# An encoder's FFN on one Trainium2 core: input normalised on the chip, eleven of 22 up chunks by seven products, convolution from PSUM, residual and some low parts by accumulating DMA

## The chip, the core and the metric

The kernel runs on one core of a Trainium2 chip. The metric is the device time of one execution in microseconds (us). The engines of the core work side by side: TensorE (PE) multiplies matrices into PSUM, VectorE (DVE) and ScalarE (ACT) work element by element, GpSimd (POOL) does small things and issues some DMAs, SyncE (SP) issues the loads. Each engine takes its instructions in a fixed order that is set when the kernel is built; semaphores make it wait for data of another engine.

## What is computed

The reference is an encoder trunk of two layers over one sequence of 512 tokens with 1024 features, in float32. Layer 0 mixes tokens by a gated linear attention, layer 1 by a grouped softmax attention with rotary positions. Each layer ends in a gated FFN with a convolution of width 3 over the tokens. Its core, cut from the reference:

```
def conv_ffn(h, w_up, w_conv, b_conv, w_down):
    u = h @ w_up                                  # 1024 -> 2 x 2816
    u = conv over 3 neighbouring tokens, one filter per feature, + b_conv
    val, gate = jnp.split(u, 2, axis=-1)
    return (jax.nn.silu(gate) * val) @ w_down     # 2816 -> 1024

x = x + mixer(rmsnorm(x, norm_mix[i]))
x = x + conv_ffn(rmsnorm(x, norm_ffn[i]), w_up[i], w_conv[i], b_conv[i], w_down[i])
```

The change bears on the FFN of both layers.

## The kernel before

**Layout.** Activations lie with features on the 128 partitions and the 512 tokens along a row, so x is eight tiles of 128 x 512 (`x[c]`, L112). Products of float32 are made from two parts of reduced width, a high part (a copy to fp32r) and a low part (the value minus its high part): `mm3` (L359) does high x high, high x low and low x high. Every weight and every activation that PE reads is thus split first, the high part by a copy on ACT, the low part by a subtraction on DVE. For some tiles the low part is made by the DMA: ACT writes the negated high part, and `flush` (L191) issues a DMA on the POOL queue that adds the full value to it (L194). The class `Weights` (L115) keeps the order of all weight pieces; `piece` (L210) hands one out and makes further ones ahead of their use. A strip is 128 x 2048 floats (1 MB), loaded on the SP queue (L136) into one of two buffers (`raw`); a piece is a quarter of the FFN's seven-product strips or half of another.

**The up projection.** An FFN has 22 chunks of 128 value features and their 128 gate features. A plain chunk (`plain_up`, L785) is two tiles, value and gate, each 8 k-steps of `mm3` with 512 columns (`feature_steps`, L365). The input is x times the norm's weight, split; the division by each token's root mean square is done afterwards, by a multiplication with `norm.R` (L803), a tile that holds this factor for every token. `act_up` (L857) then does the convolution (ACT for the middle tap and the bias, L864; DVE for the two outer taps, L865 and L866), silu on ACT (L868) and the product on DVE (L869).

**Seven products.** Six chunks a layer (SEVEN, L49) and most of the down projection use a scheme of Strassen and Winograd: a 2 x 2 block product with seven products instead of eight. Token halves of 256 columns are the blocks on one side, and pairs of 128-row blocks on the other. `seven_up` (L824) has the chunk's products; `go(i, r, ...)` runs the product i over four pairs, 12 matmuls of 128 x 256 each (`product`, L806, matmul at L815), into PSUM tiles r1 to r5. Products accumulate onto one another: r2 starts as a copy of r1, r3 as a copy of r2 (ACT, L831 and L835). `begin_up` lets a chunk's first product run inside the chunk before it. The weights' sums are made on the chip by `summed` (L151), the input's differences by `prepare_input` (L899), called after chunks 0 to 3.

**The down projection.** Chunks 0 to 15 give eight pairs, which `prepare` (L878) turns into the seven right-hand operands each. `down_part` (L921) runs after the first tile of chunk 9 for the first four pairs and of chunk 17 for the other four (DOWN_AFTER, L46), in four groups of seven products, and adds its results to x on DVE (L951, L958 to L962). Chunks 16 to 21 are multiplied plainly at the end (PLAIN, L43; L1002).

**What sets the order.** The text of the kernel gives the order of preference, and a scheduler in the build orders each engine's instructions by it and by estimated readiness. Buffers are counted by tag: PSUM has three banks of `acc`, two of `s`, two of `pt`, one of `po`; in SBUF `wh` and `wl` (split weights) have three each, beside a `ring` buffer of the size of two.

## Time and profile before

| | |
|---|---|
| device time, median of 3 runs | 1104.91 us (1104.68 to 1105.5) |
| profiled execution, first to last instruction (span) | 1103.4 us |
| profiled execution's own time | not given apart from its span; median less span is 1.5 us |
| PE busy | 1096.4 us, 6212 matmuls |
| DVE busy | 870.1 us, 1441 instructions |
| ACT busy | 633.5 us, 1034 instructions |
| POOL busy | 97.9 us |
| granted TensorE clock | 1.000 |

In the lines below, L815 is line 815 of the kernel before. A line of a group names the line, the engine, the operation, what it writes and reads by the program's names with the shape, the count, then busy us, the mean duration of one in ns, and the idle time of the engine just ahead of them with what ended it. A line of the timeline starts with the start time and the duration in us. A line of the waits gives total us, times and the longest. A line of a stretch gives its ends, its length, and for each engine busy us and the number of instructions, then the granted clock, the DMA share and GB/s. Durations of successive instructions on one engine can overlap.

### The profile page before, as it was taken

To read this page: it belongs to the slowest core of one execution; us is meant where nothing else is said; L and a number is where in the kernel's file an instruction comes from. 1 tells how busy PE (TensorE), PEld (TensorE's weight loads), DVE (VectorE), ACT (ScalarE), POOL (GpSimd) and SP (SyncE) were. 2 spreads that over 40 slices of the span, in tenths; PEclk is the share of its full clock that TensorE was granted. 3 is DMA by queue.
4 is the path that set the end of the run, shared out by engine and by line. 5 is a ranking of instruction groups with operands and counts; after the bars stand their busy time and mean duration, and the time that the engine had idled before them with its cause. 6 is when DMAs were issued, how large, how long until landed. Compare 5 with 4: busy or idle time off the path is not lost.

```text
span 1103.4 us, 16108 instructions
## 1 busy us (share of the span) xinstructions
PE 1096.4 (99%) x6212; PEld 960.6 (87%) x6212; DVE 870.1 (79%) x1441; ACT 633.5 (57%) x1034; POOL 97.9 (9%) x106
## 2 busy tenths in 40 slices
PE   9999999999999999999999999999999999999998
PEld 7888888888889988899888888788888998889987
DVE  6785775669998789987964578766999878997893
ACT  5565343446656556666664777645665655665660
POOL 0100222000000000000004343000000000000000
PEclk9999999999999999999999999999999999999999
DMA  6322222222516434364457765422151643445542
GB/s 232 134 96 89 79 100 77 77 77 80 169 45 175 129 98 140 124 173 115 140 152 182 181 178 152 163 77 81 72 166 50 167 134 97 138 129 143 145 134 77
DMA packets 33149, 136.91 MB, mean 124 GB/s; under 512 B 4016, under 2 KB 4528, under 8 KB 22704
## 3 DMA queue, kind: packets, MB, share of 16 engines
q1 hardware_dynamic: 21072, 102.16, 27.1%
q0 software_dynamic: 7104, 25.17, 11.6%
q10 hardware_dynamic: 4896, 8.55, 2.1%
q8 instruction: 49, 0.80, 0.3%
q14 instruction: 28, 0.23, 0.1%
HBM read 100.21 MB, written 2.10 MB: 93 GB/s over the span
## 4 chain that ended last, share of the span: by engine, by line
PE 92%; DVE 4%; DMA 2%; ACT 1%; issue 0%; POOL 0%; ACTq 0%; DVEq 0%; SPq 0%
PE r L815 24%; PE up L361 10%; PE up L362 10%; PE up L363 10%; PE vg L393 8%; PE op L419 8%; PE dn L363 2%; PE dn L361 2%; PE dn L362 2%; PE o L687 1%; DMA ring<-p 1%; PE av L393 1%; PE pt L1191 1%; PE A L361 1%; PE q L361 1%; PE in L620 1%
## 5 line engine op out<-in xcount | busy, mean ns | idle before, releaser
L361 PE MATMUL up<-xhl,wh 128*128 128x512 f32 x512 | 199.9, 390 | 0.0
L362 PE MATMUL up<-xhl,wh 128*128 128x512 f32 x512 | 199.5, 390 | 0.0
L363 PE MATMUL up<-xhl,wl 128*128 128x512 f32 x512 | 199.3, 389 | 0.0
L204 ACT ACTIVATE wh<-raw 128x1024 fp32r<-128x1024 f32 x108 | 114.1, 1057 | 128.8 <-PE up L362 34.0
L205 DVE TENSOR_TENSOR wl<-raw,wh 128x1024 fp32r<-128x1024 f32 x108 | 132.0, 1223 | 30.2 <-ACT wh L204 29.8
L815 PE MATMUL r<-gu,wh 128*128 128x256 f32 x640 | 116.6, 283 | 0.3 <-ACT r L950 0.3
L363 PEld LDWEIGHTS up<-xhl,wl 128*128 128x128 f32 x512 | 96.1, 188 | 20.2
L362 PEld LDWEIGHTS up<-xhl,wh 128*128 128x128 f32 x512 | 96.2, 188 | 19.2
L361 PEld LDWEIGHTS up<-xhl,wh 128*128 128x128 f32 x512 | 96.2, 188 | 19.2
L815 PEld LDWEIGHTS r<-gu,wh 128*128 128x128 f32 x640 | 99.7, 191 | 0.8 <-ACT r L950 0.5
L194 POOL DMA_DIRECT2D wl<-raw x44 | 38.9, 883 | 675.5 <-ACT r L935 195.3
L864 ACT ACTIVATE y<-u,cw 128x512 f32<-128x512 f32 x88 | 68.9, 809 | 47.4 <-DVE u L803 27.1
L815 PE MATMUL r<-gu,wl 128*128 128x256 f32 x320 | 90.4, 283 | 0.0
L393 PE MATMUL vg<-wh,xhl 128*128 128x512 f32 x256 | 80.5, 394 | 0.2 <-DVE wh L202 0.2
L865 DVE SCALAR_TENSOR_TENSOR y<-u,cw,y 128x511 f32<-128x511 f32 x88 | 64.4, 750 | 12.0 <-ACT y L864 12.0
L419 PE MATMUL op<-oT,wh 128*128 128x512 f32 x256 | 71.8, 394 | 0.6 <-ACT p L1155 0.6
L866 DVE SCALAR_TENSOR_TENSOR y<-u,cw,y 128x511 f32<-128x511 f32 x88 | 64.0, 748 | 0.5
L815 PEld LDWEIGHTS r<-gu,wl 128*128 128x128 f32 x320 | 61.1, 191 | 0.0
L393 PEld LDWEIGHTS vg<-wh,xhl 128*128 128x128 f32 x256 | 48.5, 190 | 10.5 <-ACT sq L335 0.5
L419 PEld LDWEIGHTS op<-oT,wh 128*128 128x128 f32 x256 | 47.3, 188 | 11.0 <-ACT p L1155 0.9
L815 PE MATMUL r<-xhl,wh 128*128 128x256 f32 x288 | 53.3, 283 | 0.0
L815 PE MATMUL r<-gu,ring 128*128 128x256 f32 x384 | 50.8, 281 | 0.0
(264 smaller groups left out, 2475.7 us busy)
## 6 DMA issues: line engine op xcount, KB each, us to landing
raw<-in_w_up_dram SPq DMA_DIRECT2D x42, 1024.0 KB, 4.8
wl<-raw POOLq DMA_DIRECT2D x44, 512.0 KB, 4.6
raw<-in_w_down_dram SPq DMA_DIRECT2D x22, 1024.0 KB, 4.8
raw<-in_w_vg_dram SPq DMA_DIRECT2D x6, 1024.0 KB, 4.9
ring<-p ACTq DMA_DIRECT2D x22, 256.0 KB, 3.3
raw<-in_w_kq_dram SPq DMA_DIRECT2D x4, 1024.0 KB, 4.8
raw<-in_w_gout_dram SPq DMA_DIRECT2D x4, 1024.0 KB, 4.8
raw<-in_w_aout_dram SPq DMA_DIRECT2D x16, 256.0 KB, 4.2
```

What stands on the lines that cost most here:

```text
L194: pool.dma_start(lo.bitcast(F32), r, accum_op=ALU.add)
L204: act.activation(hi[:, sl], r[:, sl], AF.Copy)
L205: dve.tensor_tensor(lo[:, sl], r[:, sl], hi[:, sl].bitcast(F32), ALU.subtract)
L361: mm(ps, wh, mh, start=start, stop=False)
L362: mm(ps, wh, ml, start=False, stop=False)
L363: return mm(ps, wl, mh, start=False, stop=stop)
L393: mm(ps[j][:, :width], hl[k][i == 2][:, j * P : (j + 1) * P], (wl if i == 1 else wh)[:, sl], start=k == 0 and i == 0, stop=k == KC - 1 and ...
L419: mm(pss[ng][n], wt[:, sl], mv, start=k == 0 and i == 0, stop=k == KC - 1 and i == 2)
L815: mm(dst, w[:, sl], m, start=start and j == 0 and a == 0, stop=j == len(pairs) - 1 and a == 2, skip_group_check=True)
L864: act.activation(y, u, AF.Identity, scale=w(1), bias=w(3))
L865: dve.scalar_tensor_tensor(y[:, 1:], u[:, : S - 1], w(0), y[:, 1:], ALU.mult, ALU.add)
L866: dve.scalar_tensor_tensor(y[:, : S - 1], u[:, 1:], w(2), y[:, : S - 1], ALU.mult, ALU.add)
```

## The change

In the FFN of each layer:

- **Input.** After chunk 0 the new `rescale` makes x times norm weight times R, four tiles of 128 x 1024, splits them (high part and negated copy on ACT, low part by accumulating DMA) and keeps them as `fresh`. Chunks 0 to 3 still use the old input and the multiplication by R; from chunk 4 on (SWITCH) the input is `fresh` and the multiplication is gone.
- **Convolution.** For those plain chunks the convolution reads the PSUM tile itself (`u = ps`).
- **Seven products.** SEVEN grows from 6 to 11 chunks: 7, 8, 10, 11, 13, 14, 16, 18 to 21. The order within a chunk becomes 6, 7, 5, 3, 4, the next chunk's first product, 2 (it was 6, 7, 2, 5, the next chunk's first, 4, 3), the gate tile is convolved ahead of the value tile, and the results need no R.
- **Differences of the input** are made in place in the scaled tiles, split by ACT and accumulating DMA, after chunks 3, 4 and 5, into buffers of the tag `xhl`.
- **Operands of the down projection**: four of the eight pairs (Q_DMA) get their low parts by DMA.
- **Residual**: a down group's results are gathered in SBUF and added to x by accumulating DMA.
- **Weights**: the third quarter of a seven-product strip gets its low part on DVE, no longer by DMA; loads come in half strips, four buffers, requested up to three pieces ahead; `wh` and `wl` have four buffers each and the `ring` buffer goes; more pieces are made ahead (UPA, PA).

In the attention layers, what used `ring` takes one buffer each of `wh` and `wl`. The diff, cut to what the prediction speaks of:

```diff
-SEVEN = (5, 11, 14, 18, 19, 21)
+SEVEN = (7, 8, 10, 11, 13, 14, 16, 18, 19, 20, 21)
+UPA = 3
+PA = 4
+LOADS = 3
+SWITCH = 4
+INPUT_AT = {3: (0, 1), 4: (2,), 5: (3,)}
+Q_DMA = (2, 4, 5, 6)
+NR = 4
+NH = 4
+NL = 4
...
+        def fetch(self, src, i, h):
+            key = (id(src), i, h)
+            if key in self.loaded:
+                return self.loaded.pop(key)
+            t = pair("raw", NR, F32, "raw")
+            n = 2 if any(src is a and i < m for a, m in self.fine) else 1
+            for q in range(n):
+                w = 2 * S // n
+                sync.dma_start(t[:, q * w : (q + 1) * w], src[i, :, h * 2 * S + q * w : h * 2 * S + (q + 1) * w])
+            return t
+        def load(self, key):
+            src, i, h = key
+            if (id(src), i) in self.sums:
+                if (id(src), i) not in self.strip:
+                    self.strip[id(src), i] = [self.fetch(src, i, 0), self.fetch(src, i, 1)]
+            else:
+                k = (id(src), i, h)
+                if k not in self.loaded:
+                    self.loaded[k] = self.fetch(*key)
...
+        def low_dma(self, hi, lo, r):
+            act.activation(hi, r, AF.Copy)
+            act.activation(lo, r, AF.Copy, scale=-1.0)
+            self.pending.append((lo, r))
...
             if h == 1:
                 dve.tensor_tensor(a11, a21, a11, ALU.add)
-                r = raw[:, : 2 * S]
-            elif h == 2:
-                r = raw[:, 2 * S :]
-            else:
-                r = tmp("sq", "sum4")
-                dve.tensor_tensor(r, a11, a12, ALU.add)
-                hi, lo = (sp.tile([P, S], F32R, tag="sq", bufs=3, name=nm(n)) for n in ("wh4", "wl4"))
-                act.activation(hi, r, AF.Copy)
-                self.last = dve.tensor_tensor(lo, r, hi.bitcast(F32), ALU.subtract)
+                hi, lo = self.two()
+                self.split(hi, lo, t1)
                 return hi, lo
-            if h == 1:
-                t = sp.tile([P, 4 * S], F32R, tag="ring", bufs=1, name=nm("ring"))
-                hi, lo = t[:, : 2 * S], t[:, 2 * S :]
-            else:
-                hi, lo = pair("wh", 3, F32R, "wh"), pair("wl", 3, F32R, "wl")
             if h == 2:
-                act.activation(hi, r, AF.Copy)
-                act.activation(lo, r, AF.Copy, scale=-1.0)
-                self.pending.append((lo, r))
-            else:
-                act.activation(hi, r, AF.Copy)
-                dve.tensor_tensor(lo, r, hi.bitcast(F32), ALU.subtract)
+                hi, lo = self.two()
+                self.split(hi, lo, t3)
+                return hi, lo
+            r = tmp("sq", "sum4")
+            dve.tensor_tensor(r, a11, a12, ALU.add)
+            hi, lo = (sp.tile([P, S], F32R, tag="sq", bufs=3, name=nm(n)) for n in ("wh4", "wl4"))
+            act.activation(hi, r, AF.Copy)
+            self.last = dve.tensor_tensor(lo, r, hi.bitcast(F32), ALU.subtract)
...
+            for key in self.todo[:LOADS]:
+                self.load(key)
...
+        scaled, fresh = [], []
+        def rescale():
+            for p in range(KC // 2):
+                xr = big(F32, "xr")
+                for i in range(2):
+                    c = 2 * p + i
+                    dve.scalar_tensor_tensor(xr[:, i * S : (i + 1) * S], x[c], norm.weight(c), norm.R, ALU.mult, ALU.mult)
+                hi, lo = big(F32R, "nh"), big(F32R, "nl")
+                W.low_dma(hi, lo, xr)
+                scaled.append(xr)
+                fresh.extend((hi[:, i * S : (i + 1) * S], lo[:, i * S : (i + 1) * S]) for i in range(2))
         def plain_up(m):
             pss = []
             for t in range(2):
                 ps = bank("s" if t else "acc", "up")
-                feature_tile(*W.half(up[layer], 2 * m + t, ahead.get((m, t), 1)), norm.hl, ps)
+                feature_tile(*W.half(up[layer], 2 * m + t, max(UPA, ahead.get((m, t), 1))), norm.hl if m < SWITCH else fresh, ps)
                 pss.append(ps)
                 if t == 0 and m not in DOWN_AFTER:
                     begin_up(m + 1)
@@ -798,15 +837,18 @@
                     norm.tokens()
                 elif m == 0:
                     norm.rows()
-            for ps in pss:
-                u = tmp("u", "u")
-                dve.tensor_tensor(u, ps, norm.R, ALU.mult)
-                yield u
+                    rescale()
+            for t, ps in enumerate(pss):
+                u = ps
+                if m < SWITCH:
+                    u = tmp("u", "u")
+                    dve.tensor_tensor(u, ps, norm.R, ALU.mult)
+                yield t, u
         def product(pieces, src, strip, pairs, i, dst, start):
             h, o = PLACE[i]
             if h not in pieces:
-                pieces[h] = W.piece(src, strip, h, 3)
+                pieces[h] = W.piece(src, strip, h, PA)
             wh, wl = pieces[h]
             for j, p in enumerate(pairs):
                 sl = slice(o + j * P, o + (j + 1) * P)
@@ -835,43 +877,44 @@
             act.activation(r3, r2, AF.Copy)
             r4 = bank("pt", "r4")[:, :H]
             go(7, r4, True)
-            go(2, r1, False)
-            c, d = tmp("u", "u"), tmp("u", "u")
-            dve.tensor_tensor(c[:, :H], r1, norm.R[:, :H], ALU.mult)
             go(5, r2, False)
-            begin_up(m + 1)
-            go(4, r3, False)
             r5 = bank("pt", "r5")[:, :H]
             go(3, r5, True)
-            act.activation(d[:, :H], r4, AF.Copy)
-            act.activation(d[:, H:], r4, AF.Copy)
-            dve.tensor_tensor(d[:, H:], d[:, H:], r2, ALU.add)
-            dve.tensor_tensor(d[:, :H], d[:, :H], r3, ALU.add)
+            c, d = tmp("u", "u"), tmp("u", "u")
+            two = lambda a: a.rearrange("p (o t) -> p o t", t=H)
+            act.activation(two(d), two(r4).to_broadcast([P, 2, H]), AF.Copy, scale=-1.0)
+            dve.tensor_tensor(d[:, H:], d[:, H:], r2, ALU.subtract)
             act.activation(c[:, H:], r5, AF.Copy)
             dve.tensor_tensor(c[:, H:], c[:, H:], r2, ALU.add)
-            dve.tensor_tensor(c[:, H:], c[:, H:], norm.R[:, H:], ALU.mult)
-            yield c
-            dve.scalar_tensor_tensor(d, d, -1.0, norm.R, ALU.mult, ALU.mult)
-            yield d
+            go(4, r3, False)
+            begin_up(m + 1)
+            go(2, r1, False)
+            dve.tensor_tensor(d[:, :H], d[:, :H], r3, ALU.subtract)
+            yield 1, d
+            act.activation(c[:, :H], r1, AF.Copy)
+            yield 0, c
...
+            far = p in Q_DMA
+            split(y2, t[1], by_dma=far)
+            split(y1, t[0], by_dma=far)
             dve.scalar_tensor_tensor(q[:, H:], b12, -1.0, b22, ALU.mult, ALU.subtract)
-            split(q, t[2])
-            dve.scalar_tensor_tensor(b21, q[:, H:], -1.0, b21, ALU.mult, ALU.subtract)
+            split(q, t[2], by_dma=far)
+            b4 = sp.tile([P, S], F32, tag="R", bufs=1, name=nm("b4"))[:, :H] if far else b21
+            dve.scalar_tensor_tensor(b4, q[:, H:], -1.0, b21, ALU.mult, ALU.subtract)
             o = (p % 2) * H
-            split(b21, t4, o, H)
+            split(b4, t4, o, H, by_dma=far)
...
         def prepare_input(p):
-            y1, y2, q = (tmp("t", n) for n in ("x1", "x2", "q"))
-            for i, y in enumerate((y1, y2)):
-                act.activation(y, x[2 * p + i], AF.Copy, scale=norm.weight(2 * p + i))
-            b11, b12, b21, b22 = y1[:, :H], y1[:, H:], y2[:, :H], y2[:, H:]
-            dve.tensor_tensor(q[:, :H], b22, b12, ALU.subtract)
-            dve.tensor_tensor(b12, b11, b12, ALU.subtract)
-            t = [big(F32R, "xt") for _ in range(2)]
-            split(b12, t[0], 0, H)
-            dve.scalar_tensor_tensor(q[:, H:], b12, -1.0, b22, ALU.mult, ALU.subtract)
-            split(q, t[1])
-            dve.scalar_tensor_tensor(b21, q[:, H:], -1.0, b21, ALU.mult, ALU.subtract)
-            split(b21, t[0], H, H)
-            half = lambda a, i: (a[:, i : i + H], a[:, S + i : S + i + H])
-            whole = lambda k, i: tuple(a[:, i : i + H] for a in norm.hl[k])
-            inputs.append({1: whole(2 * p, 0), 5: half(t[0], 0), 2: whole(2 * p + 1, 0), 3: whole(2 * p + 1, H),
-                           7: half(t[1], 0), 6: half(t[1], H), 4: half(t[0], H)})
+            y = scaled[p]
+            b11, b12, b21, b22 = (y[:, n * H : (n + 1) * H] for n in range(4))
+            dve.tensor_tensor(b11, b11, b12, ALU.subtract)
+            dve.tensor_tensor(b12, b22, b12, ALU.subtract)
+            dve.scalar_tensor_tensor(b22, b11, -1.0, b22, ALU.mult, ALU.subtract)
+            dve.scalar_tensor_tensor(b21, b22, -1.0, b21, ALU.mult, ALU.subtract)
+            hi, lo = pair("xhl", 8, F32R, "xt"), pair("xhl", 8, F32R, "xt")
+            W.low_dma(hi, lo, y)
+            part = lambda n: (hi[:, n * H : (n + 1) * H], lo[:, n * H : (n + 1) * H])
+            whole = lambda k, i: tuple(a[:, i : i + H] for a in fresh[k])
+            inputs.append({1: whole(2 * p, 0), 5: part(0), 2: whole(2 * p + 1, 0), 3: whole(2 * p + 1, H),
+                           7: part(1), 6: part(3), 4: part(2)})
         PLACE = {1: (0, S), 7: (0, 0), 6: (1, S), 5: (1, 0), 2: (2, 0), 4: (2, S), 3: (3, 0)}
@@ -944,22 +985,23 @@
                 act.activation(r3, r2, AF.Copy)
                 r4 = bank("pt", "r4")[:, :H]
                 go(n, 7, r4, True)
-                go(n, 2, r1, False)
                 go(n, 5, r2, False)
-                r5 = tmp("u", "r5", H)
-                act.activation(r5, r2, AF.Copy)
-                dve.tensor_tensor(c[:, :H], c[:, :H], r1, ALU.add)
+                two = lambda a: a.rearrange("p (o t) -> p o t", t=H)
+                g, f = tmp("u", "g"), tmp("u", "f")
+                act.activation(two(f), two(r4).to_broadcast([P, 2, H]), AF.Copy, scale=-1.0)
+                dve.tensor_tensor(f[:, H:], f[:, H:], r2, ALU.subtract)
                 go(n, 4, r3, False)
+                dve.tensor_tensor(f[:, :H], f[:, :H], r3, ALU.subtract)
+                W.pending.append((d, f))
+                go(n, 3, r2, False)
+                act.activation(g[:, H:], r2, AF.Copy)
                 if n + 1 < NQ:
                     begin(n + 1)
                 else:
                     begin_up(m + 1)
-                two = lambda a: a.rearrange("p (o t) -> p o t", t=H)
-                dve.tensor_tensor(two(d), two(d), two(r4).to_broadcast([P, 2, H]), ALU.subtract)
-                dve.tensor_tensor(d[:, H:], d[:, H:], r5, ALU.subtract)
-                dve.tensor_tensor(d[:, :H], d[:, :H], r3, ALU.subtract)
-                go(n, 3, r2, False)
-                dve.tensor_tensor(c[:, H:], c[:, H:], r2, ALU.add)
+                go(n, 2, r1, False)
+                act.activation(g[:, :H], r1, AF.Copy)
+                W.pending.append((c, g))
...
-            if m < KC // 2:
-                prepare_input(m)
+            for p in INPUT_AT.get(m, ()):
+                prepare_input(p)
```

77 lines of the change are left out of this document (38 added, 39 removed).

## The prediction, before the result was known

> **What bounds the kernel now.** I read the head of the page first, then the chain that ended last, then whom TensorE (PE) waited for, then the busy time by stage.
>
> ```profile
> span 1103.4 us, 16108 instructions
> PE 1096.4 (99%) x6212; PEld 960.6 (87%) x6212; DVE 870.1 (79%) x1441; ACT 633.5 (57%) x1034; POOL 97.9 (9%) x106
> PE 92%; DVE 4%; DMA 2%; ACT 1%; issue 0%; POOL 0%; ACTq 0%; DVEq 0%; SPq 0%
> ```
>
> PE is busy for all but 7 us, and 92% of the chain is its own work. The span is 1103.4 us, 1.5 us under the median of the three runs (1104.91); I take these 1.5 us as lying around the span and unchanged. Sums below are made on the span and carried to the median.
>
> PE's waits for other engines, all but two at the start of the kernel:
>
> ```profile
> PE op L419 <- ACT p L1155: 0.6, 1, 0.6
> PE pt L1191 <- DMA ring<-p: 0.6, 1, 0.6
> PE r L815 <- ACT r L950: 0.3, 1, 0.3
> PE po L362 <- DVE ptl L1194: 0.2, 1, 0.2
> ```
>
> Three of the four rows (1.4 us) are of the attention. In 28 groups of seven products and 32 plain chunks of the FFN, PE waited 0.3 us in all. So time leaves this kernel only if PE has less to do, and it comes back only if something makes PE wait. The engine most likely to do that is VectorE (DVE). The stages of layer 0 below are chunks 0 to 9, then (after a down part) chunks 10 to 17, the second down part, and chunks 18 to 21; after the length come PE, PEld, DVE, ACT and POOL busy us:
>
> ```profile
> 225.66:339.00 113.34, 113.34 (x562) 96.29 (x561) 104.32 (x175) 69.14 (x106) 2.86 (x3) 1.00 0.31 96
> 380.00:462.40 82.40, 82.40 (x450) 71.83 (x450) 72.44 (x115) 47.39 (x72) 2.62 (x3) 1.00 0.38 116
> 462.40:503.00 40.60, 40.60 (x342) 40.60 (x342) 34.28 (x58) 26.14 (x41) 3.48 (x4) 1.00 0.60 160
> 503.00:543.50 40.50, 40.50 (x291) 38.32 (x291) 35.78 (x57) 26.60 (x43) 1.74 (x2) 1.00 0.51 151
> ```
>
> DVE is busy 92% of the first stage, and PE still never waits there: weights are split ahead. In the down part PEld is busy 100%: with 256 columns a matmul is as short as its weight load.
>
> **PE: the only term that pays.** Pitch, not duration, counts, since matmuls overlap. From the PE timeline (two starts 24 matmuls apart in a plain chunk) and the chain (492 matmuls of 256 columns in a row):
>
> ```profile
> 241.36 0.39 PE L361 MATMUL up<-xhl,wh 128*128 128x512 f32 x1
> 246.80 0.39 PE L361 MATMUL up<-xhl,wh 128*128 128x512 f32 x1
> 462.39 58.74 PE r L815 x492
> ```
>
> 512 columns: 5.44 / 24 = 0.2267 us. 256 columns: 58.74 / 492 = 0.1194 us. A plain chunk is 2 tiles x 8 x 3 = 48 matmuls, 10.88 us. A chunk of seven products is 7 x 4 pairs x 3 = 84, 10.03 us. The change turns five more chunks in each of two layers from plain to seven: 10 x 0.85 = **8.5 us less**. The number and shape of all other matmuls stays; the products of a group are only put in another order.
>
> **DVE: moved, not lightened.** Its pitch in a stretch without idle time:
>
> ```profile
> 523.14 1.22 DVE L205 TENSOR_TENSOR wl<-raw,wh 128x1024 fp32r<-128x1024 f32 x1
> 524.28 0.41 DVE L848 TENSOR_TENSOR u<-u,r 128x256 f32<-128x256 f32 x1
> 524.61 0.41 DVE L849 TENSOR_TENSOR u<-u,r 128x256 f32<-128x256 f32 x1
> ...
> 526.21 0.69 DVE L876 TENSOR_TENSOR gu<-y,gu 128x512 fp32r<-128x512 f32 x1
> 526.81 0.69 DVE L166 TENSOR_TENSOR raw<-raw 128x512 f32<-128x512 f32 x1
> 527.41 1.41 DVE L865 SCALAR_TENSOR_TENSOR y<-u,cw,y 128x511 f32<-128x511 f32 x2
> 528.73 1.41 DVE L866 SCALAR_TENSOR_TENSOR y<-u,cw,y 128x511 f32<-128x511 f32 x2
> ```
>
> Starts give 1.14 us for 1024 columns, 0.33 for 256, 0.60 for 512, 0.66 for a convolution tap (1.32 for two). By chunk:
> - Plain, before: 2 splits, 2 multiplications by R, 4 taps, 1 product: 2.28 + 1.20 + 2.64 + 0.60 = 6.72. From chunk 4 on the change drops the two multiplications: 5.52.
> - Seven, before: weights 7 x 0.60 + 1.14 = 5.34, outputs 5 x 0.33 + 0.60 = 2.25, taps and product 3.24: 10.83. After: the third piece's low part returns from the DMA to DVE, so weights cost 6.48; R is gone, outputs are 3 x 0.33 = 0.99; with 3.24 that is 10.71.
> - A pair prepared for the down part: 5 x 0.33 + 3 x 0.60 = 3.45 on DVE; the four pairs sent by DMA cost 4 x 0.33 = 1.32.
> - A down group: 6.48 + 2 x 0.33 = 7.14 (before 5.34 + 0.60 + 4 x 0.33 = 7.26), of 10.03 us of PE.
>
> Chunks 10 to 17 checked against the trace: 2 sevens, 6 plain, 3 pairs and 2 plain splits make 21.66 + 40.32 + 10.35 + 1.20 = 73.5, and the row, which begins some 5 us into chunk 10, says 72.44. After: 5 x 10.71 + 3 x 5.52 + 2 x 1.32 + 3.45 + 1.20 = **77.4 us against 5 x 10.03 + 3 x 10.88 = 82.8 of PE, 93%**, about the first stage's 92% now. Chunks 18 to 21: 4 x 10.71 + 2.4 = 45.2, less one strip (6.48) split during the down part (28.6 of 40.1 busy): 38.8 of 40.1. That is tight, but the last chunks' taps may run on: the final products reach them 16 x 3 x 0.2267 = 10.9 us later. The first stage gets lighter: the multiplications by R of chunks 4 to 6 and the input preparation (8 x 0.66 for the new scaled input and 16 x 0.33, 10.6 us, as much as before) now spread over chunks 0 to 5, and chunk 5 is plain.
>
> Taps now read PSUM in seven chunks a layer. The rows nearest to this, a tap-like operation from PSUM and the tap from SBUF:
>
> ```profile
> L1046 DVE SCALAR_TENSOR_TENSOR rt<-A,prm,rope 128x512 f32<-128x512 f32 x10 | 7.0, 747 | 6.6 <-ACT qa L1036 6.6
> L865 DVE SCALAR_TENSOR_TENSOR y<-u,cw,y 128x511 f32<-128x511 f32 x88 | 64.4, 750 | 12.0 <-ACT y L864 12.0
> ```
>
> Equal, so I cost it at nothing. The PSUM bank is held until the taps are done instead of one multiplication; the same tag is wanted again only a whole chunk (10 us) later.
>
> **POOL, DMA, ACT.**
>
> ```profile
> L194 POOL DMA_DIRECT2D wl<-raw x44 | 38.9, 883 | 675.5 <-ACT r L935 195.3
> wl<-raw POOLq DMA_DIRECT2D x44, 512.0 KB, 4.6
> L950 ACT ACTIVATE r<-r 128x256 f32<-128x256 f32 x16 | 5.9, 367 | 0.0
> L204 ACT ACTIVATE wh<-raw 128x1024 fp32r<-128x1024 f32 x108 | 114.1, 1057 | 128.8 <-PE up L362 34.0
> ACT y L868 <- DVE y L866: 35.6, 22, 2.6
> SPq L136 <- DVE wl L205: 556.0, 53, 26.0
> ```
>
> Accumulating DMAs go from 14 to 40 a layer (4 scaled inputs, 4 differences, 16 for four pairs, 16 residual adds): 40 x 0.88 = 35 us of POOL in some 350, and POOL has 675 us idle. Issue and landing make 5.5 us. Residual tiles are wanted again two down groups (20 us) later; the pairs' low parts a dozen us later at the earliest. The tightest is the last input pair: 4 x 0.33 + 2 x 1.06 + 5.5 = 8.9 us after chunk 5, against 5.44 + 1.43 + 5.44 = 12.3 until the sixth product reads it (a tile, one product of 12 matmuls, a tile). On the POOL queue a DMA that waits for its source holds up only other such DMAs. SP now issues weight loads as half strips, twice as many of half the size; its queue does nothing else in these stages and stands 556 us waiting for a free buffer, so this is free too, and a half is freed earlier than a strip was. All this I cost at nothing; without that cover it is some us once a layer.
>
> What can bite is ACT in front of PE. In the new order the copy of r1 into r2 has only one product (12 x 0.1194 = 1.43 us) between its input and the matmul that needs it, as in the down parts now, where it cost 0.3 us in 16. The copy takes 0.37; a split of 1.06 begun just before makes 1.43, just covered. But ACT also stands behind DVE's taps (22 waits, longest 2.6 us), and DVE is now nearly full beside these copies. Bounds for 22 sevens: nothing, and 1.5 us each. I take 0.05 us each, near the 0.3 in 16: **1.1 us**.
>
> Sum: -8.5 + 1.1 = -7.4 on the profiled span, 1096.0, and **1097.5 us** as a median.
>
> **Rivals.**
> 1. *Part of it is eaten by ACT and DVE in the runs of sevens.* The 2.6 us wait of ACT on DVE, less 1.43 of cover, is 1.2 us; if one seven in five meets it, PE loses 0.24 x 22 = 5.3 us: 1104.9 - 8.5 + 5.3 = 1101.7. It decides where DVE's queue is late at the copy r1 to r2. For it: 93 to 97% DVE. Against: 92% without a wait now.
> 2. *DVE becomes the bound: slower.* If it cannot overlap its operations and each costs its duration (1.22, 0.69, 0.75, 0.42), a seven is 7 x 0.69 + 2 x 1.22 + 3 x 0.42 + 4 x 0.75 + 0.69 = 12.2, a plain chunk 6.1; chunks 10 to 17 need 88.4 against 82.8, chunks 18 to 21 some 44.4 against 40.1: 9.9 us a layer, 19.8 - 8.5 = +11.3, 1116. It decides once the mean pitch is 82.8 / 77.4 = 1.07 of the one I read, or once waits on raw weights and ACT leave DVE idle as much. Against: the starts 526.21 and 526.81, 0.60 apart for 0.69 long. [...]
> 3. *More than forecast.* If the weights loaded earlier, in halves, also end the 1.4 us of waits in the attention and no seven waits, it is 1104.9 - 8.5 - 1.4 = 1095.0. If 256 columns took half of 512's pitch in the new chunks, 84 x 0.1134 = 9.52, they would save 13.6 us: 1091.3. Against that: PEld at 100%, and 0.1194 in every run of them. [...]
> 4. *The change doesn't do what it says*: if the 256-column pitch in the new chunks were 48 x 0.2267 / 84 = 0.1295 instead of 0.1194, nothing would be saved (1104.9). The row of 492 such matmuls speaks against it; I count it with rival 1.
>
> **Chances.** Forecast (1095.5 to 1100) 0.56; rival 1 with 4 (1100 to 1106) 0.20; rival 2 (1106 to 1120) 0.18; rival 3 (below 1095.5) 0.06, of it 0.01 for the half pitch. A difference of 0.2%, 2.2 us, is about what a measurement of this kernel can tell. Of rival 1 about two thirds lie below 1102.7. Faster 0.76, same 0.07, slower 0.17. Range: 1095 to 1108, which leaves out most of rival 2 and the lower part of rival 3.
>
> **What would show it.** Right: PE idle still under 10 us, 256-column matmuls 0.119 us apart, DVE 92 to 97% in chunks 10 to 17, no PE wait on an ACT r copy above 1 us. Rival 1: PE waits on ACT r copies or DVE low parts adding to 4 to 7 us. Rival 2: DVE at 20 of 20 us through chunks 10 to 16 and PE waits of over 10 us on DVE's low parts (wl). What would make me wrong: instructions of DVE or ACT in another order than their data come, which no row of the kernel before can show.

## The result, and the profile after

The changed kernel takes **1100.49 us** (median of 4, 1099.92 to 1100.92) against 1104.80 for the kernel before beside it: a ratio of 0.9958 [0.9944, 0.9973]. In a second measurement (below) it was 0.9943 [0.9929, 0.9956]. The prediction was 1097.5, faster, in a range of 1095 to 1108: the sign and the main term held, and 1.4 to 3.1 us of the forecast gain did not come. The first median lies half a microsecond above the band of the forecast (1095.5 to 1100), in that of rival 1; the second, 1098.78, lies in it.

The head of its page, and the first rows of PE's waits:

```profile
span 1098.1 us, 17393 instructions
PE 1091.6 (99%) x6572; PEld 974.3 (89%) x6572; DVE 872.0 (79%) x1397; ACT 672.5 (61%) x1142; POOL 143.4 (13%) x158
```

```profile
PE vg L419 <- DVE wh L225: 0.6, 1, 0.6
PE pt L1233 <- DMA ring<-p: 0.5, 1, 0.5
```

PE is still busy 99%, and no row of its waits belongs to the FFN. So the shape of the bound is as before; only PE's work changed. To see where, the chain of waits has one mark per stage, the eight small matmuls that sum a norm (start, us, what). First before, then after:

```profile
28.18 0.79 PE ms L347 x8
...
231.26 0.79 PE ms L347 x8
...
585.66 0.79 PE ms L347 x8
...
755.39 0.79 PE ms L347 x8
```

```profile
29.98 0.79 PE ms L373 x8
...
233.30 0.79 PE ms L373 x8
...
585.26 0.79 PE ms L373 x8
...
753.57 0.79 PE ms L373 x8
```

| stage | before | after | difference |
|---|---|---|---|
| start, first projection | 28.18 | 29.98 | +1.80 |
| linear attention | 203.08 | 203.32 | +0.24 |
| FFN of layer 0 (before the marks are rounded) | 354.39 | 351.96 | -2.43 |
| attention | 169.73 | 168.31 | -1.42 |
| FFN of layer 1 (to the end; from the first ms matmul itself) | 348.13 | 344.73 | -3.40 |
| span | 1103.4 | 1098.1 | -5.2 |

The two FFN stages give **5.83 us**, the rest adds up to +0.6. An FFN stage is a good measure: in four executions that differ at most in the warm-up, it was 351.96 to 351.97 and 344.71 to 344.73. The tables below therefore compare stages, each from one profiled execution; whole times also hold a start that varies by up to 2.8 us (27.45 to 30.26 us until the first mark; last section).

DVE in the tight stages of layer 0 (chunks 10 to 17, the second down part, chunks 18 to 21), columns as in the windows of before:

```profile
380.00:462.00 82.00, 81.97 (x553) 75.91 (x552) 75.30 (x118) 58.84 (x103) 10.46 (x12) 1.00 0.52 138
462.00:503.00 41.00, 41.00 (x342) 40.87 (x341) 33.93 (x51) 24.60 (x44) 6.02 (x7) 1.00 0.54 138
503.00:543.50 40.50, 40.50 (x330) 40.02 (x329) 38.76 (x59) 29.91 (x52) 0.86 (x1) 1.00 0.43 129
```

DVE is busy 92%, 83% and 96%; the prediction had 93% and 97% for the first and the third. PE loses 0.03 us in the first.

### The profile page after: what moved, and what is told of

Read it like the earlier page. It is cut to its first block, busy times and chain, and to the rows that moved or that the text cites. A ratio compares the mean times of both kernels' runs of the same rounds, so it can differ in the third digit from the quotient of the medians.

```text
span 1098.1 us, 17393 instructions
## 1 busy us (share of the span) xinstructions
PE 1091.6 (99%) x6572; PEld 974.3 (89%) x6572; DVE 872.0 (79%) x1397; ACT 672.5 (61%) x1142; POOL 143.4 (13%) x158
## 4 chain that ended last, share of the span: by engine, by line
PE 98%; DMA 1%; DVE 0%; ACT 0%; issue 0%; SPq 0%; DVEq 0%; ACTq 0%
PE r L857 35%; PE vg L419 8%; PE op L445 8%; PE up L387 7%; PE up L388 7%; PE up L389 7%; PE dn L387 2%; PE dn L389 2%; PE dn L388 2%; PE av L419 1%; PE o L713 1%; PE A L387 1%; PE A L389 1%; PE B L387 1%; PE B L389 1%; PE A L388 1%
## 5 line engine op out<-in xcount | busy, mean ns | idle before, releaser
L228 DVE TENSOR_TENSOR wl<-raw,wh 128x1024 fp32r<-128x1024 f32 x164 | 199.9, 1224 | 47.9 <-ACT wh L227 46.2
L857 PE MATMUL r<-xt,wh 128*128 128x256 f32 x704 | 129.3, 284 | 0.1
L857 PEld LDWEIGHTS r<-xt,wh 128*128 128x128 f32 x704 | 109.8, 192 | 1.5 <-ACT r L877 0.5
L857 PE MATMUL r<-xt,wl 128*128 128x256 f32 x352 | 99.0, 283 | 0.0
L387 PE MATMUL up<-nh,wh 128*128 128x512 f32 x224 | 87.4, 390 | 0.0
L388 PE MATMUL up<-nl,wh 128*128 128x512 f32 x224 | 87.4, 390 | 0.0
L389 PE MATMUL up<-nh,wl 128*128 128x512 f32 x224 | 87.1, 389 | 0.0
L419 PE MATMUL vg<-wh,xhl 128*128 128x512 f32 x256 | 81.1, 396 | 0.6 <-DVE wh L225 0.6
L857 PE MATMUL r<-nh,wl 128*128 128x256 f32 x264 | 74.7, 283 | 0.0
L857 PE MATMUL r<-nl,wh 128*128 128x256 f32 x264 | 74.7, 283 | 0.0
L857 PE MATMUL r<-nh,wh 128*128 128x256 f32 x264 | 74.7, 283 | 0.0
```

The lines of the kernel that those rows point to most:

```text
L228: dve.tensor_tensor(lo[:, sl], r[:, sl], hi[:, sl].bitcast(F32), ALU.subtract)
L387: mm(ps, wh, mh, start=start, stop=False)
L388: mm(ps, wh, ml, start=False, stop=False)
L389: return mm(ps, wl, mh, start=False, stop=stop)
L419: mm(ps[j][:, :width], hl[k][i == 2][:, j * P : (j + 1) * P], (wl if i == 1 else wh)[:, sl], start=k == 0 and i == 0, stop=k == KC - 1 and ...
L857: mm(dst, w[:, sl], m, start=start and j == 0 and a == 0, stop=j == len(pairs) - 1 and a == 2, skip_group_check=True)
```

## The experiments

**Theory:** ten more chunks of the two layers by seven products give about 0.8 us each on PE; DVE has just room for them; the rest of the change makes that room and pays nothing itself. **Rivals:** the other parts pay too; or it is not DVE's load that limits but a transfer, or the look-ahead, or ACT's queue.

All FFN stages in one table (us). "Need" is DVE's need in chunks 10 to 17 by the pitches of the prediction, over PE's time there. "DVE" and "ACT" are their busy time from 380 to 462 us, which is about these chunks. A lull is a gap of over 128 ns between the starts of two successive matmuls of 256 columns; "lulls" sums what these gaps have beyond 120 ns in the FFN of layer 0.

| kernel | need | DVE | ACT | lulls | FFN of layer 0 | FFN of layer 1 |
|---|---|---|---|---|---|---|
| before | 73.5 of 85.3 (86%) | 72.4 | 47.2 | 0 | 354.39 | 348.13 |
| list of eleven alone, in the old code | 85.9 of 82.8 (104%) | 73.9 | 53.4 | 12.1 | 363.05 | 359.28 |
| changed, list of six | 61.8 of 85.3 (72%) | 60.8 | 46.8 | 0.4 | 355.29 | 348.05 |
| **changed** | 77.4 of 82.8 (93%) | 75.3 | 58.8 | 1.13 | 351.96 | 344.73 |
| copies from PSUM | 81.0 of 82.8 (98%) | 76.6 | 59.7 | 2.52 | 353.30 | 345.29 |
| residual and pairs on DVE | 81.7 of 82.8 (99%) | 79.7 | 55.1 | 0.64 | 351.53 | 344.29 |
| twelve | 82.6 of 81.9 (101%) | 77.8 | 61.4 | 2.54 | 352.51 | 345.16 |
| thirteen | 87.8 of 81.1 (108%) | 78.5 | 64.2 | 6.03 | 355.15 | 348.14 |
| third low part by DMA | 71.7 of 82.8 (87%) | 66.9 | 61.1 | 3.76 | 357.56 | 353.33 |
| short look-ahead | as changed | 74.6 | 56.4 | 0.82 | 351.68 | 344.70 |
| other order at product 4 | as changed | 74.1 | 59.2 | 1.35 | 352.21 | 344.92 |

### The changed kernel again

No edit. 

> The changed kernel once more, unedited. Its profile spent 1.8 us more than the kernel before up to the end of the first 96 matmuls, because its matmuls were 426 ns apart until 10.54 us (before: until 7.12 us) and the first weights landed 0.4 us later. [...] Rival: a lasting cost of the change; then the step is at 10.5 us again, with the first weights later than 5.6 us.

Measured: 1098.78 (1097.61 to 1100.52) against 1104.77; 0.9943 [0.9929, 0.9956]; FFN stages 351.97 and 344.73. The gain is there in both measurements, 4.3 and 6.0 us. The step to the full rate fell at 10.46 us again and the first matmul of the projection began at 5.74, both as the rival had; but the median is 1.7 us lower, where the author had estimated 1100.5 within 0.8 for a step that comes early or late by chance. That the late step is no fixed cost of the change is read from other kernels (last section), not from this run.

### The list alone, in the old code

```diff
-SEVEN = (5, 11, 14, 18, 19, 21)
+SEVEN = (7, 8, 10, 11, 13, 14, 16, 18, 19, 20, 21)
```

> The kernel before with the new list of eleven seven-product chunks and nothing else of the change. Theory (the rest of the change pays for the sevens on VectorE): chunks 10 to 17 need 5 x 10.83 + 3 x 6.72 + 3 x 3.45 + 1.2 = 85.9 us of VectorE against 82.8 of TensorE and chunks 18 to 21 some 40 against 40, so TensorE waits some 3 us a layer and the gain of 8 us shrinks to 2: about 1103, with VectorE full in these stages. Rival (the matmul count alone does it, VectorE's queue is elastic): 1104.8 - 5.8 = 1099, as fast as the whole change or faster. Second rival (four split-weight buffers too few for runs of sevens): slower than before, over 1107, with TensorE waiting on the split weights.

Measured: 1126.41 against 1104.77, ratio 1.0196 [1.0182, 1.021]: 21.6 us slower, as the second rival said (over 1107, with PE waiting on split weights). PE's waits, and a window in chunks 10 to 17:

```profile
PE r L815 <- DMA wl<-raw: 9.0, 10, 1.7
PE r L815 <- ACT r L831: 3.8, 2, 1.9
PE r L815 <- DVE wl L163: 1.7, 3, 1.2
```

```profile
385.00:470.00 85.00, 82.03 (x543) 74.38 (x542) 77.79 (x133) 53.62 (x88) 3.48 (x4) 1.00 0.41 115
```

PE idles 3 us of these 85, yet DVE is busy only 92%, the same share at which the changed kernel loses nothing. What PE waits for most is the low part that an accumulating DMA makes (`wl<-raw`). DVE's load can be a part of this: by the pitches its need is 104%, between twelve's 101% and thirteen's 108%. But those lists lose some 1.3 and 5 us a layer against what their chunks should bring (0.85 us each), and this one some 13 and 15, so a late transfer, or what it holds, weighs more; the experiment on the third quarter, below, tries that alone. The second rival's cause, too few buffers of split weights, was tried by no run.

### The rest without the list

```diff
-SEVEN = (7, 8, 10, 11, 13, 14, 16, 18, 19, 20, 21)
+SEVEN = (7, 11, 14, 18, 19, 21)
```

(in the changed kernel). 

> The changed kernel with six seven-product chunks (7, 11, 14, 18, 19, 21) in place of eleven: all else of the change stays. Theory (only the count pays, the rest costs TensorE 1 to 3 us by shorter lulls and a slower pitch): the changed kernel plus 10 x (48 x 0.2273 - 84 x 0.1206) = +7.8, 1108.3 at 1100.5, slower than the kernel before by 2 to 4. Rival (the lulls come with the runs of sevens, the rest is free): as the kernel before, 1104.8 within 1.

Measured: 1105.43 against 1104.77, ratio 1.0011 [1.0002, 1.0021]: within 1 us of the kernel before, as the rival said. Its marks:

```profile
230.83 0.79 PE ms L373 x8
...
586.12 0.79 PE ms L373 x8
```

The FFN of layer 0 is 355.29: the rest of the change alone costs 0.9 us in layer 0 and 0.1 less in layer 1. From here to eleven chunks it is -3.33 and -3.32: **6.65 us for ten chunks, 0.67 each.** The whole gain in the FFN is the list's, given the rest of the change.

### Two more chunks: thirteen

`SEVEN` with 12 and 15. 

> Chunks 12 and 15 are done by seven products too (thirteen a layer). By the pitches on record VectorE then needs 7 x 10.71 + 5.52 + 2.64 + 3.45 + 1.2 = 87.8 us in chunks 10 to 17 against 7 x 10.03 + 10.88 = 81.1 of TensorE. Theory (VectorE is a hard bound just above the 92% seen now): the FFN stages, 351.96 and 344.73 us in the changed kernel, get 3 to 6 us longer each, with TensorE waiting for low parts of weights in chunks 13 to 17. Rival (what VectorE does ahead of its time absorbs the excess): each gets about 1.2 us shorter, less about 0.3 of lulls.

Measured: 355.15 and 348.14, longer by 3.2 and 3.4; 1106.44 in one run.

```profile
PE r L857 <- ACT r L873: 3.1, 4, 0.8
...
PE r L857 <- ACT wh L195: 2.0, 2, 1.1
PE r L857 <- ACT wh L210: 1.4, 2, 0.7
```

```profile
380.00:462.00 82.00, 79.71 (x618) 76.76 (x617) 78.50 (x129) 64.20 (x116) 10.47 (x12) 1.00 0.50 126
```

DVE is up from 75.30 to 78.50 busy, 96%, and PE idles 2.3 us in this window. The theory's size came; its waits did not: PE is released by ACT, not by low parts of DVE. Four gaps of over 1 us make up 3.7 of the 6.0 us of lulls in layer 0. In front of each, ACT had worked for 2 us or more without a pause, and what ended its idle time before that was PE; the next section shows such a gap. So these rows do not show a late DVE: they show a queue on ACT.

### One more: twelve

`SEVEN` with 12. 

> Chunk 12 is done by seven products too (twelve a layer; chunk 15 stays plain). By the pitches on record VectorE needs 6 x 10.71 + 2 x 5.52 + 2.64 + 3.45 + 1.2 = 82.6 us in chunks 10 to 17 against 81.9 of TensorE. Theory (the bound is where these cross): the loss takes back what the chunk saves, each FFN stage within 1 us of 351.96 and 344.73. Rival (what is ahead of time absorbs it): each 0.6 to 0.85 us shorter.

Measured: 352.51 and 345.16, longer by 0.55 and 0.43. 1098.59 in one run, its start 1.9 us earlier than in the changed kernel's profile. The chunk should have saved some 0.8; lulls rose from 1.13 to 2.54 and 2.48 us a layer. The loss came at twelve, where the pitches have DVE's need cross PE's time, and of the lists tried eleven is the best. But the crossing is not shown to be the cause. About 1 us of the new lulls in each layer is one wait, for the copy of r1 into r2 (L873). ACT's and PE's timelines in layer 0:

```profile
401.65 0.63 ACT L908 ACTIVATE y<-y 128x512 f32<-128x512 f32 x1 [1.21 <-DVE y L906]
402.91 0.38 ACT L887 ACTIVATE u<-r 128x256 f32<-128x256 f32 x1 [0.63 <-PE r L857]
...
409.04 0.40 ACT L180 ACTIVATE gu<-b 128x256 fp32r<-128x256 f32 x1
...
410.39 0.36 ACT L873 ACTIVATE r<-r 128x256 f32<-128x256 f32 x1
```

```profile
410.80 0.51 PE L857 MATMUL r<-xt,wh 128*128 128x256 f32 x2 [0.74 <-ACT r L873]
```

From 402.91 to the copy ACT has no idle time. Eight of its operations in that stretch (L179, L180) are the high parts and negated copies of a pair whose low parts go by DMA. ACT's last wait for DVE ended at 401.65, and behind it ACT waited 0.63 us for PE, so that wait did not make the copy late. This is the mechanism of rival 1, at the copy that it named.

### The third quarter's low part by DMA again

```diff
             if h == 2:
                 hi, lo = self.two()
-                self.split(hi, lo, t3)
+                self.low_dma(hi, lo, t3)
```

> The third quarter's low part is made again by a ScalarE copy and an accumulating DMA instead of by VectorE; eleven chunks by seven products, and all the rest as in the changed kernel. VectorE gets some 20 us lighter a layer, ScalarE some 18 us heavier. Theory (the part that comes back some 5 us after its issue, and the raw buffer that it holds meanwhile, are what broke the list of eleven in the old kernel): FFN stages longer by 3 us or more each than 351.96 and 344.73, with TensorE waiting for a DMA into wl. Rival (VectorE's load broke it): as long as in the changed kernel or shorter.

Measured: 357.56 and 353.33, longer by **5.6 and 8.6 us**; 1114.35 in one run, slower than before. And this with DVE 38.6 us lighter (833.4 busy). The theory's times came; its wait, for a DMA into wl, is the smaller one. A window, then PE's first waits, then a stretch of the chain:

```profile
380.00:462.00 82.00, 78.77 (x543) 73.03 (x542) 66.86 (x110) 61.09 (x105) 13.85 (x16) 1.00 0.69 166
```

```profile
PE r L857 <- ACT r L873: 7.0, 3, 3.9
PE r L857 <- DMA wl<-raw: 1.9, 4, 0.7
```

```profile
389.61 6.39 DMA wl<-raw
396.05 4.48 DMA raw<-in_w_up_dram
400.61 1.07 ACT wh L227
```

and ACT's and PE's timelines just behind it:

```profile
400.61 1.06 ACT L227 ACTIVATE wh<-raw 128x1024 fp32r<-128x1024 f32 x1 [5.46 <-DMA raw<-in_w_up_dram]
...
408.84 1.05 ACT L179 ACTIVATE wh<-raw 128x1024 fp32r<-128x1024 f32 x1
409.79 1.04 ACT L180 ACTIVATE wl<-raw 128x1024 fp32r<-128x1024 f32 x1
...
414.46 0.36 ACT L873 ACTIVATE r<-r 128x256 f32<-128x256 f32 x1
```

```profile
414.88 0.51 PE L857 MATMUL r<-xt,wh 128*128 128x256 f32 x2 [2.83 <-ACT r L873]
```

DVE has 15 us to spare in 82, and PE idles 3.2. The accumulating DMA reads `raw` for 6.39 us; only then may the next weights be loaded into that buffer, 4.48 us; for these ACT stands idle 5.46 us. Afterwards its queue is full of copies, two for each part whose low part goes by DMA (from 408.84 on, two of the third quarter and then eight of a pair), and r1's copy, on which PE waits 2.83 us, comes behind them. One edit puts two things at once, a buffer held longer and a heavier ACT, and this stretch has both; how they share the loss is open.

Layer 1 loses 3 us more. There PE waits 3.94 us for the same copy, and in the stretch below, from 942.80 to 946.10 us, the granted clock is 0.50:

```profile
943.10 0.58 PE L857 MATMUL r<-xt,wh 128*128 128x256 f32 x1 [3.94 <-ACT r L873]
```

```profile
942.80:946.10 3.30, 3.00 (x14) 3.00 (x15) 2.32 (x4) 2.79 (x6) 1.41 (x2) 0.50 1.08 181
```

Its 14 matmuls of 256 columns in 3.00 us are some 214 ns apart instead of 120, by these figures an estimated 1.3 us lost. Of all parts of the change beside the list, this one (the low part on DVE) is shown to be needed. The buffers, the half strips and the new order within a chunk were not taken back one by one.

### Copies from PSUM before the convolution

```diff
                 if m < SWITCH:
...
+                else:
+                    u = tmp("u", "u")
+                    dve.tensor_copy(u, ps)
```

> Plain chunks from 4 on copy their tiles from PSUM to SBUF on VectorE again before the taps (instead of the multiplication by R that the changed kernel dropped): 14 tiles of 0.60 us, 8.4 us of VectorE a layer more. Theory (the spare VectorE time hides it): FFN stages within 0.5 us of 351.96 and 344.73. Rival (reading PSUM in the taps is what lets eleven chunks pay): each longer by 2 us or more.

Measured: +1.34 and +0.56; 1103.02 in one run. This is between the two, in layer 1 only just above the theory's 0.5. Most of the loss in layer 0 is one wait of PE, 0.8 us for a high part that ACT makes (L195); ACT itself had waited 0.85 us for DVE some 3 us before it, so here a late DVE can stand behind ACT's name. 8.4 us of DVE a layer cost a sixth and a fifteenth of that. Reading PSUM directly is worth 1.9 us in all, a third of the gain, but not a condition of it.

### Residual and pairs on DVE

```diff
-Q_DMA = (2, 4, 5, 6)
+Q_DMA = ()
...
-                W.pending.append((d, f))
+                dve.tensor_tensor(d, d, f, ALU.add)
...
-                W.pending.append((c, g))
+                dve.tensor_tensor(c, c, g, ALU.add)
```

> The accumulating DMAs for the residual (16 a layer) and for the low parts of four pairs (16 a layer) are taken back: VectorE does them again, 9.6 and 8.5 us a layer more, in the old order of the work. Lists of eleven and all else as in the changed kernel. VectorE then needs about 81.7 of 82.8 us in chunks 10 to 17 and 39.3 of 40.1 in a down part. Theory (just under the bound costs little, as with the copies from PSUM): FFN stages longer by 0.5 to 3 us each than 351.96 and 344.73. Rival A (these DMAs are needed for eleven chunks): longer by over 4 us each. Rival B (they bring nothing): within 0.5 us.

Measured: 351.53 and 344.29, **shorter** by 0.43 and 0.44; 1098.08 in one run, span 1095.9 (its start was also 2.1 us earlier). No expectation had that; rival B, that these DMAs bring nothing, is the nearest. Its page and the window:

```profile
PE 1088.7 (99%) x6572; PEld 972.4 (89%) x6572; DVE 903.3 (82%) x1461; ACT 660.2 (60%) x1110; POOL 88.1 (8%) x94
```

```profile
380.00:462.00 82.00, 82.00 (x557) 76.25 (x556) 79.72 (x129) 55.05 (x91) 0.00 (x0) 1.00 0.31 103
```

DVE is busy 97% and PE loses nothing. ACT falls from 58.84 to 55.05: an accumulating DMA needs the high part and its negative, two ACT copies instead of one. The lulls fall from 1.13 to 0.64 us. DVE at 97% is harmless here. That a lighter ACT is what gained is likely and not shown alone, for the transfers went with its copies. In the table the lulls of the kernels with eleven to thirteen chunks in the new code rise with ACT's busy time, but for one pair; by DVE's busy time the lightest kernel and the fullest one break the order. Twelve or thirteen chunks with the pairs on DVE, which no run has, would tell ACT's queue from DVE's need. By stages this is the best kernel of the study, 0.9 us better than the changed one; its whole time was measured once only.

### Short look-ahead

`UPA = 1`, `PA = 3`. 

> Weights are made no further ahead than in the old kernel (one half strip for the plain chunks and three for the products, where the changed kernel asks for three and four). Theory (with VectorE at 92% and more its jitter needs the look-ahead): each FFN stage longer by 2 us or more than 351.96 and 344.73, with TensorE waiting for low parts. Rival (only the mean load of VectorE counts): within 0.5 us.

Measured: 351.68 and 344.70, no longer, as the rival said; 1100.77 in one run. The theory fell: the deeper look-ahead, costed at nothing in the prediction, is worth nothing.

### Another order, and two more warm-up matmuls

```diff
-            go(4, r3, False)
             begin_up(m + 1)
+            go(4, r3, False)
             go(2, r1, False)
...
     for i in range(8):
         mm(warm[:, :P], ...
+    for i in range(2):
+        mm(warm[:, P : 2 * P], two[:, :P], two[:, P : 2 * P], start=i == 0, stop=i == 1)
```

> In a chunk of seven products the first product of the next chunk goes ahead of product 4 instead of behind it (so that two products, 2.86 us, lie between the sum of 6 and its copy and the matmuls that need the copy), and two more warm-up matmuls as in the earlier run. Theory (the lulls of about 0.15 us at product 4, and the lost runs of fast pairs beside them, are TensorE waiting for ScalarE's copy): the lulls at 256 columns fall from 1.13 us to under 0.6 a layer and each FFN stage gets 0.4 to 1 us shorter than 351.96 and 344.73. Rival (they are spread over other causes): within 0.2 us. The start goes as in the earlier run with two more matmuls.

Measured: 352.21 and 344.92 (+0.25 and +0.19, about the rival), lulls 1.35 and 1.34 us: no better, and the theory of product 4 fell. A stretch of the timeline of the changed kernel shows why:

```profile
390.92 0.62 ACT L908 ACTIVATE y<-y 128x512 f32<-128x512 f32 x1
...
391.42 0.28 PE L857 MATMUL r<-nh,wh 128*128 128x256 f32 x1
...
391.44 0.36 ACT L877 ACTIVATE r<-r 128x256 f32<-128x256 f32 x1
391.54 0.28 PE L857 MATMUL r<-nl,wh 128*128 128x256 f32 x1
...
391.85 0.30 PEld L857 LDWEIGHTS r<-xt,wh 128*128 128x128 f32 x2 [0.23 <-ACT r L877]
391.85 0.51 PE L857 MATMUL r<-xt,wh 128*128 128x256 f32 x2
```

ACT's copy of r2 to r3 (L877) comes behind a silu in ACT's queue, begins at 391.44 and ends at 391.80; PE resumes at 391.85. The twelve `xt` matmuls that begin there are product 5, which goes on adding into r2, the very bank being copied. (The build's scheduler has put two matmuls of product 3 in front.) The wait, 0.23 us in the row of the weight load, is for the **reader of the bank**, one product of 1.43 us after the sum of 6, and moving product 4 does not touch it. The old order had two products there, 7 and 2.

### More warm-up

Both on the changed kernel: ten warm-up matmuls instead of eight, and eight with the two of the last diff.

> The changed kernel with ten warm-up products at the start in place of eight, so that TensorE works on until 5.5 us, when the first weights land, and has no idle 0.4 to 1 us there. [...]

> Two more warm-up matmuls ahead of the first projection, into other columns of the same bank, their value unused. [...]

With ten in one sum the exponent of the norms, read from that bank, is -0.625 instead of -0.5, so that kernel's output is not the reference's; the second kernel leaves the exponent as it is. Measured: 1098.57 (0.9944 [0.9932, 0.9957]) and 1099.04 (0.9939 [0.9925, 0.9952]); the order above had 1098.78 (0.9940 [0.9927, 0.9954]). For both edits the author had estimated the step by 7.2 us, as before (7.12), in place of 10.54, and a median lower by 0.5 to 1.4 us with ten and by 0.5 to 2 us with the two, taking PE's idle time ahead of the projection (0.64 us in the changed kernel, 0.22 before) for what sets the step. In all three profiles the first matmuls at full rate begin at 7.1 to 7.3 us, about as estimated; but the medians, 0.9939 to 0.9944 against 0.9943 of the unedited kernel, show no gain. As a way to a faster kernel it fell.

## Why the prediction was right, and where it missed

**PE, -8.5 us: right in kind, measured 6.65.** That is the stage of eleven chunks against that of six in the changed code. The chain of the changed kernel has

```profile
337.98 53.84 PE r L857 x446
...
462.08 79.63 PE r L857 x660
```

that is 0.1207 us a matmul, not 0.1194 (the figure of one run of 492 in layer 0; the mean over layer 1 before was already 0.1202). With some 3200 such matmuls, 0.8 ns more each than the 0.1198 of both layers before are 2.5 us: 8.5 less 2.5 is 6.0, and the FFN stages gave 5.83.

**ACT in front of PE, +1.1 us: near in size, by luck, and at another copy.** These 2.5 us have two parts, 2.6 by a count of gaps. Lulls add up to 2.27 us in the two layers, before 0.94: +1.33, close to the term. But in the up chunks none of over 0.01 us stands at the copy r1 to r2, where the prediction put them. Some 1.4 us of the 2.27 stand at product 5 of the up chunks, behind the copy r2 to r3, and the rest mostly in the down parts. The step that the prediction missed is in its own list of products: the order was 6, 7, 2, 5 and became 6, 7, 5, so the copy r2 to r3 lost one of the two products (1.43 of 2.86 us) that covered it, and no term has that. The other 1.28 us are not in any term either, and are what was mis-sized in PE's: before, 28% of the gaps were 112 to 119 ns, 1.87 us in all under the common 120; after, 0.59 us. No wait goes with that. The old code with the list of eleven has them too (1.37 us a layer), the new code has few with any list (0.16 us with six, 0.10 to 0.31 with eleven), so they went with the rest of the change, not with the list; 0.8 us of them in layer 0 are most of the 0.9 us that it costs there. What made them stays open.

**DVE, moved and not lightened, costed at nothing: right.** 92% and 96% busy where 93% and 97% were worked out, and no row of PE's waits. Beyond that the losses begin where the pitches put the crossing: twelve chunks, 101%, lose slightly, thirteen, 108%, lose 4.9 us a layer (3.2 and the 1.7 that two chunks should have saved). But there PE waits for ACT's copies, and copies from PSUM (98%) cost 0.6 to 1.3 while the adds on DVE (99%) cost nothing, so DVE's need alone does not set the limit.

**Rival 2, DVE the bound, 1116: out for eleven chunks.** It needed a mean pitch 1.07 times the one read; thirteen chunks bring the same ratio by more work and do lose, but with PE waiting for ACT. With durations for pitches eleven would have lost 9.9 us a layer and lost none, so DVE's operations overlap here as the starts said, 0.60 us apart for operations 0.69 long: each begins 0.09 us before the end of the one ahead.

**Convolution from PSUM, at no extra cost: right.** 

```profile
L905 DVE SCALAR_TENSOR_TENSOR y<-u,cw,y 128x511 f32<-128x511 f32 x60 | 43.6, 745 | 2.8 <-ACT y L904 2.6
L905 DVE SCALAR_TENSOR_TENSOR y<-up,cw,y 128x511 f32<-128x511 f32 x28 | 20.6, 745 | 10.0 <-ACT y L904 10.0
```

745 ns from SBUF (`u`) and from PSUM (`up`).

**Accumulating DMAs, free: nearly.** PE waits for none of them in the changed kernel; what is not free is more likely the second ACT copy of each low part. Taking 32 of 40 a layer back, copies and all, gains 0.9 us in two layers.

**Moving the third low part to DVE, only counted (+1.14 a strip): under-read.** The prediction listed it as a cost of DVE and did not see that the old code could not carry the list. The 675 us of POOL's idle time and the 5.5 us of latency were read as free; what counts is the buffer held meanwhile (6.39 us in the stretch above) and ACT's second copy (1.04 us there), 5.6 and 8.6 us together (an estimated 1.3 of the second at the half clock).

**Rivals 1 and 4.** Rival 1 named ACT's copies and came for a quarter of its price (1.3 of 5.3 us), at another copy; at twelve and thirteen chunks it came at the copy that it named. Rival 4 is out: the pitch in new chunks is 0.1207, not 0.1295.

**Rival 3, waits of the attention gone (-1.4).** That stage is 1.42 shorter, and 168.06 to 169.33 in the nine profiles of the changed code with eleven chunks, so 0.4 to 1.7 below the one profile of before (169.73). Of the waits that the prediction listed, the two on `op` and `po` (0.8 us) are gone and the one on a DMA (`pt`) is still there, 0.5 us. A gain is likely, its size not settled.

**What the sum left out: the start.** +1.80 us, by no part of the change that the runs single out.

## What to carry to other kernels

Where one engine is the bound, as PE was here at 99%, count the other engines' pitches stage by stage: the stage in which the second engine's need crosses the first one's time is the place to look for the end of the trade. Here it ended at that place, after eleven chunks, but the waits named a third engine, ACT, at 61 of 82 us: the copy that PE needed was late where a block of other copies stood in front of it (eight of a pair with twelve chunks, where PE waited 0.74 us; ten with the third quarter's low part by DMA, 2.83 us). An accumulating DMA spared VectorE an instruction here, but it cost ScalarE a second copy (in chunks 10 to 17, 103 instructions and 58.84 us of ACT against 91 and 55.05 with the pairs' low parts on DVE) and held its source buffer until it had landed (6.39 us, and 4.48 for the next load into it); look for the load that wants that buffer, and for what stands behind the copy. And read a wait's bank, not only its tile: here a copy of 0.36 us out of an accumulator held up the next product that adds into the same one, by 0.23 us in the stretch shown.

## What the runs showed of the hardware that was not expected

**The full rate at the start came in one of three spans of time.** The first projection's matmuls of 512 columns are 427 ns apart until some moment, and 227 ns after it. The timeline of PE at the start of the changed kernel, and of the kernel with two more warm-up matmuls:

```profile
5.72 2.04 PE L419 MATMUL vg<-wh,xhl 128*128 128x512 f32 x4 [0.64 <-DVE wh L225]
7.56 1.91 PE L419 MATMUL vg<-wl,xhl 128*128 128x512 f32 x4
```

```profile
5.97 1.73 PE L421 MATMUL vg<-wh,xhl 128*128 128x512 f32 x4
7.54 1.09 PE L421 MATMUL vg<-wl,xhl 128*128 128x512 f32 x4
```

Four matmuls in 1.91 us, against four in 1.09. The moment was 5.7 to 6.4 us in four profiles (there all but the first matmul go at the full rate), 7.1 to 7.3 in four (before among them) and 10.2 to 11.1 in six (the changed kernel among them). Executions that begin with the same instructions, on one chip, fall into the first group (twelve, adds on DVE) and the third (short look-ahead), so it is no fixed property of the code, though both profiles of the changed kernel itself are in the third. Before, matmuls went at the slow rate from 5.30 to 7.12 us, in the changed kernel from 5.72 to 10.54: 3.0 us more at about half rate, which loses 1.4 us, and a first matmul 0.42 us later are the 1.80 us of the start. What sets the moment was not shown. The profile's own PEclk shows 1.00 from 4 to 8 and from 8 to 12 us, before and after, all the same.

**With a wait of PE of 3.94 us came half the clock.** In the run with the third low part by DMA, PE idled from about 939.2 to 943.1 us, and from 942.80 to 946.10 the granted clock was 0.50 (lines above). In layer 0, with a wait of 2.83 us, it was 1.00 from 380 to 462 us. One such case does not show what made the clock fall.

**This lull cost more than its wait.** The matmul after the one that waited also came 0.22 us later instead of 0.12 (391.85, then 392.07; the two take 0.51 us, two without a lull 0.40): the wait above, 0.19 us beyond the usual 0.12, cost 0.29.
